# A two-block transformer layer stack on one core: the HGRN recurrence handled by halves of four heads

## The chip, the core and the metric

The kernel runs on one core of a Trainium2 chip. Its time is the device time of one execution in microseconds (us), the median over the runs shown. The engines are TensorE (PE), VectorE (DVE), ScalarE (ACT), GpSimd (POOL) and SyncE (SP); each works through its own queue in order and waits for the others at semaphores.

## What is computed

256 tokens of width 1024 in float32 pass through two blocks. Block 1 has two layers: a sparse attention (called DSA below) and an HGRN mixer, each followed by a residual layer norm and a SwiGLU feed-forward with its own layer norm. Block 2 (MIX) has gated linear attention beside latent attention, and a last feed-forward. The mixer around which the change is made, cut to what matters:

```
q, f, i, g = split(x @ w_in)                 # each 256 x 1024, 8 heads of 128
q  = silu(q);  fg = lb + (1 - lb) * sigmoid(f)
k  = 1 - fg;   logf = log(fg)
# per head, t the query's token, s <= t the key's:
b = cumsum(logf);  attn[t, s] = sum_d q[t, d] * exp(b[t, d] - b[s, d]) * k[s, d]
o = attn @ i  (+ what the state of earlier chunks adds)
o = rms_norm(o, g_norm) * silu(g)
return o @ w_o
rms_norm(x, g)      = x * rsqrt(mean(x*x) + eps) * g
layer_norm(x, g, b) = (x - mean) * rsqrt(var + eps) * g + b
```

## The kernel before, in words

The tokens are two tiles t = 0, 1 of 128 rows. Matrix products keep float32 accuracy by splitting each operand into a high part (`hi`, what the matmul's input format holds) and a low part (`lo`, the rest): `mm3` (L208 to L212) issues three matmuls, hi x hi (L210), hi x lo (L211) and lo x hi (L212). Weights come in units of 512 KB (`unit`, L183): SP issues the transfer into the ring `raw` of 4 buffers (L188), ACT rounds it into `rhi` (L174), and DVE (L176) or, for the names in `ON_POOL`, POOL in four pieces (L181) subtracts to get `rlo`. `rhi` and `rlo` have 9 buffers each. SP starts a transfer when a buffer of `raw` is free, in the order of use, so a held buffer holds up all weights behind it.

The stages in the order of time are DSA (to about 130 us of the span), the first feed-forward (to 327), HGRN (to about 500), the second feed-forward, MIX and the last feed-forward. Each stage is a string of steps (`HGRN`, `MIX`, ...) that `run` calls in turn; a scheduler then orders each engine's queue by its own estimates, so an edit in one place can reorder neighbours in another.

`hgrn_consts` (L696) runs beside the first feed-forward. It loads three tables through POOL's queue (L152) into buffers of the ring `raw`: `sel`, `lev`, and one that holds `msk`, `suf` and `id64`. DVE copies the last two out at L709 to L717, PE reads `sel` at L705.

In HGRN a projection step `P.x.t` is 8 `mm3` of 512 columns into one PSUM bank, evacuated by ACT or DVE. `l.t` takes logarithms of f and splits them; `t.t` forms q x k (`qk`, POOL, L761), sums it into the diagonal `dg` (L762), and turns q and k into `qT` and `kT` by PE transposes. `p.t.i` is a pair of heads: PE multiplies the logarithms with the table `lev` (L807, L808), ACT takes the exponential `e` (L810), and at each of the levels l = 0 to 6 the late halves of blocks of e are multiplied with `qT` (L817, DVE) and the early halves with `kT` (L819, DVE, or POOL at levels 2 and 5). PE then forms the products of a level (L824, L830), DVE places them under a mask into `blocks` (L835) and copies `attn` (L224), and PE multiplies by i (L846). The order before takes eleven projections, then the first pairs; five projections stand beside or between the eight pairs.

`rstd` (L254) makes 1/sqrt(scale x s + eps) on POOL in two instructions, a multiply-add (L257) and a power (L258). `rstd_halves` (L891) does it for a sum held in two parts, with two multiply-adds (L897, L898) and a power (L899); ACT squares the halves (L270) first, and DVE multiplies by the root at L910.

## Time and profile before

| | |
|---|---|
| median of 3 runs | 1157.36 us (1154.54 to 1159.5) |
| profiled execution, its own time | 1154.16 us |
| its span | 1152.4 us (1.76 us lie outside) |
| granted TensorE clock, mean | 0.989 of full speed |
| busy: PE, DVE, ACT, POOL | 1106.6, 697.3, 583.9, 224.3 us |

The profile is of one execution. Windows cut its span into stretches and give the busy time of each engine in them; a stretch less PE's busy time is PE's idle time there. The views of waits say which instruction an engine was waiting for, how long in total, how often, and the longest; a timeline shows each instruction with its start, its duration and, in brackets, the idle time of the engine just before it.

### The profile page before, as it was taken

The page shows a single profiled execution, that of the slowest core. Times are in us where ns is not written, and L with a number is a line of the kernel's source. Part 1 is how long each engine was busy: PE and PEld are TensorE (multiplying, and loading weights), DVE is VectorE, ACT ScalarE, POOL GpSimd, SP SyncE. Part 2 cuts the span into 40 slices and gives each one's busy share as a digit, 9 for nine tenths or more (in the row PEclk, how much of TensorE's full clock was granted, in tenths as well). Part 3 has the DMA queues.
Part 4 walks back from the last instruction along what each step waited for, and adds up shares of the span by engine and source line. Part 5 has one row for each costly group of instructions (what it writes and reads, how often), then busy time and mean ns, then how long its engine had stood idle before and what let it go on. Part 6 is the DMA issues. An engine that isn't in the chain of part 4 may idle for free.

```text
span 1152.4 us, 15343 instructions
## 1 busy us (share of the span) xinstructions
PE 1106.6 (96%) x5724; PEld 903.0 (78%) x5724; DVE 697.3 (61%) x1061; ACT 583.9 (51%) x832; POOL 224.3 (19%) x336
## 2 busy tenths in 40 slices
PE   8779999999999999999999999999999999999997
PEld 6546888878888777788888887887788878888886
DVE  6986755535566677875545486446655547454542
ACT  5656455525467466444444346763546456453441
POOL 2800620000432223200000022534100181000000
...
GB/s 250 159 85 5 243 166 229 182 119 255 146 146 173 103 145 77 119 214 180 218 183 192 175 131 174 207 159 102 164 192 146 146 146 225 174 222 202 171 140 37
DMA packets 98458, 187.33 MB, mean 163 GB/s; under 512 B 9400, under 2 KB 26952, under 8 KB 98384
## 3 DMA queue, kind: packets, MB, share of 16 engines
...
q14 instruction: 29, 0.24, 0.1%
HBM read 185.28 MB, written 1.05 MB: 162 GB/s over the span
## 4 chain that ended last, share of the span: by engine, by line
PE 81%; DVE 8%; POOL 4%; DMA 3%; issue 2%; ACT 2%; SPq 0%; POOLq 0%; DVEq 0%; ACTq 0%
PE a L210 15%; PE a L211 15%; PE a L212 15%; PE y L211 8%; PE y L210 8%; PE y L212 8%; PE t L236 3%; POOL rlo L181 2%; DVE rlo L176 1%; PE lv L830 1%; DMA raw<-in_ffn_w_up_dram 1%; DMA raw<-in_ffn_w_gate_dram 1%; DVE m L381 1%; ACT rhi L174 1%; PE L L538 1%
## 5 line engine op out<-in xcount | busy, mean ns | idle before, releaser
L176 DVE TENSOR_TENSOR rlo<-raw,rhi 128x1024 fp32r<-128x1024 f32 (+4 forms) x306 | 370.2, 1215 | 216.3 <-ACT rhi L174 204.8
L174 ACT ACTIVATE rhi<-raw 128x1024 fp32r<-128x1024 f32 (+3 forms) x338 | 352.7, 1047 | 242.8 <-PE y L212 75.5
L210 PE MATMUL a<-rhi,xh 128*128 128x512 f32 (+4 forms) x840 | 318.6, 379 | 3.4 <-ACT sil L625 1.8
L211 PE MATMUL a<-rlo,xh 128*128 128x512 f32 (+4 forms) x840 | 316.7, 377 | 0.2 <-DVE rlo L176 0.2
L212 PE MATMUL a<-rhi,xl 128*128 128x512 f32 (+4 forms) x840 | 315.4, 376 | 0.0
L210 PEld LDWEIGHTS a<-rhi,xh 128*128 128x128 f32 x840 | 158.7, 189 | 32.1 <-ACT xh L174 2.0
L211 PEld LDWEIGHTS a<-rlo,xh 128*128 128x128 f32 x840 | 158.8, 189 | 27.8 <-DVE rlo L176 0.6
L212 PEld LDWEIGHTS a<-rhi,xl 128*128 128x128 f32 x840 | 158.8, 189 | 27.4
L181 POOL TENSOR_TENSOR rlo<-raw,rhi 128x256 fp32r<-128x256 f32 x128 | 99.2, 811 | 179.8 <-ACT rhi L174 179.7
L210 PE MATMUL y<-rhi,hth 128*128 128x512 f32 x264 | 104.7, 396 | 0.5 <-ACT hth L174 0.5
L212 PE MATMUL y<-rhi,htl 128*128 128x512 f32 x264 | 103.2, 391 | 0.0
L211 PE MATMUL y<-rlo,hth 128*128 128x512 f32 x264 | 102.9, 390 | 0.0
L210 PE MATMUL y<-rhi,xh 128*128 128x512 f32 (+2 forms) x152 | 59.1, 390 | 3.1 <-ACT rhi L174 3.1
L257 POOL TENSOR_SCALAR rv<-mv 128x1 f32<-128x1 f32 x10 | 7.2, 716 | 272.0 <-DVE mv L266 271.8
L211 PE MATMUL y<-rlo,xh 128*128 128x512 f32 (+2 forms) x152 | 59.0, 388 | 1.0 <-POOL rlo L181 0.6
L212 PE MATMUL y<-rhi,xl 128*128 128x512 f32 (+2 forms) x152 | 58.6, 387 | 0.0
L174 ACT ACTIVATE hth<-t 128x512 fp32r<-128x512 f32 (+1 forms) x36 | 20.1, 558 | 75.6 <-PE t L236 75.6
L210 PEld LDWEIGHTS y<-rhi,hth 128*128 128x128 f32 x264 | 49.6, 188 | 10.7 <-ACT hth L174 1.1
L212 PEld LDWEIGHTS y<-rhi,htl 128*128 128x128 f32 x264 | 49.5, 188 | 10.6
L211 PEld LDWEIGHTS y<-rlo,hth 128*128 128x128 f32 x264 | 49.6, 188 | 9.7
L631 DVE TENSOR_TENSOR sil<-a,sil 128x512 f32<-128x512 f32 (+1 forms) x36 | 23.2, 643 | 51.1 <-PE a L212 51.0
L625 ACT ACTIVATE sil<-a 128x512 f32<-128x512 f32 (+1 forms) x36 | 20.2, 561 | 58.9 <-PE a L212 58.8
...
## 6 DMA issues: line engine op xcount, KB each, us to landing
...
```

The costliest lines, as they stand in the source:

```text
L174: self.nc.scalar.activation(hi, src, AF.Copy)
L176: self.nc.vector.tensor_sub(lo, src, hi.bitcast(F32))
L181: eng.tensor_sub(lo[:, c], src[:, c], hi[:, c].bitcast(F32))
L210: mm(out, xh, wh, start=start, stop=False)
L211: mm(out, xh, wl, start=False, stop=False)
L212: mm(out, xl, wh, start=False, stop=stop)
L236: self.nc.tensor.transpose(tp[:, j, :], b, self.ident)
L381: e2.tensor_tensor(m2, v[:, :, ::-1, :], s[:, None, :, :].to_broadcast(sh), ALU.mult)
L538: nc.tensor.matmul(L[:, j : j + 2, :], qT[t][:, g * 4 + (h0 + j) // 2, :], kT[:, g, :, :nk], start=False, stop=j == per - 2,)
L625: nc.scalar.activation(sil[ci, t][:, :cn], a[:, :cn], AF.Silu)
L631: nc.vector.tensor_mul(sil[ci, t][:, :cn], a[:, :cn], sil[ci, t][:, :cn])
L830: nc.tensor.matmul(lv[64 * c : 64 * c + 64, l - l0, j, :32], y, late, start=True, stop=True)
```

## The change

The recurrence is cut by halves n of four heads: logarithms, q x k and the transposes are steps of one (t, n). f and q of a half share one tile `fq`, and k and q transposed share one tile `QK`. At a level the two multiplies become one over the whole 128 tokens of each head: its second operand (`asked`) takes, every 64 >> l elements, k's and then q's values in turn from `QK`. All four logarithm steps stand together, pairs begin after eight projections, and one projection follows each pair. `h_k2`, `h_k5` and `hgrn_q1` leave `ON_POOL`, so the low parts of q1's four weight units go to DVE. The three tables of `hgrn_consts` go into tiles of the pool `w4` (10 buffers) instead of `raw`. In `rstd` the scale moves into ACT's squaring, the addition of eps to DVE in place; POOL keeps the power. In `rstd_halves` one DVE instruction adds both halves and eps.

```diff
@@ -251,12 +251,15 @@
         return X
 
 
-    def rstd(self, s, src, n, scale, eps):
-        v = self.sm(s, n, name="rv")
+    def root(self, s, v, n):
         r = self.sm(s, n, name="rs")
-        self.nc.gpsimd.tensor_scalar(v, src, scale, eps, ALU.mult, ALU.add)
         self.nc.gpsimd.tensor_tensor(r, v, self.nhalf[:, :n], ALU.pow)
         return r
+
+    def rstd(self, s, src, n, eps):
+
+        self.nc.vector.tensor_scalar(src, src, eps, None, ALU.add)
+        return self.root(s, src, n)
 
     def meanvar(self, s, views):
...
-    def sumsq(self, s, src, dst, junk):
-        self.nc.scalar.activation(junk[:, : src.shape[-1]], src, AF.Square, accum_out=dst)
+    def meansq(self, src, dst, junk, n):
+
+        self.nc.scalar.activation(junk[:, : src.shape[-1]], src, AF.Square, scale=n ** -0.5, accum_out=dst)
...
-        nc.scalar.activation(sq, o, AF.Square)
+        nc.scalar.activation(sq, o, AF.Square, scale=d ** -0.5)
...
-        raw = lambda: self.tile("raw", (P, 1024), F32, "raw")
-        sel = self.load(raw()[0:8, :], self.const("sel", 8)).rearrange("p (a b) -> p a b", a=8)
+        stage = [self.w4(name="stage") for _ in range(3)]
+        sel = self.load(stage[0][0:8, :], self.const("sel", 8)).rearrange("p (a b) -> p a b", a=8)
...
-        nc.vector.tensor_copy(lev, self.load(raw(), self.const("lev")))
+        nc.vector.tensor_copy(lev, self.load(stage[1], self.const("lev")))
         msk = self.w1(1, (P, 6, 32), mybir.dt.uint8, name="msk")
         o, n = OFF["msk"]
-        both = self.load(raw()[:, : n + P + 64], self.consts[:, o : o + n + P + 64])
+        both = self.load(stage[2][:, : n + P + 64], self.consts[:, o : o + n + P + 64])
...
+                both = self.w4(name="fq")
+                fg[t, n], q[t, n] = both[:, :512], both[:, 512:]
+                o = fg[t, n]
...
+        def logs(t, n):
+
+            if n not in lf:
+                lf[n] = (self.tile("rhi", (P, 2, 512), F32R, "lfh"), self.tile("rlo", (P, 2, 512), F32R, "lfl"))
+            x = self.w2(t, name="lf")
+            nc.scalar.activation(x, fg[t, n], AF.Ln)
+            self.halves(lf[n][0][:, t, :], lf[n][1][:, t, :], x)
+            nc.vector.tensor_scalar(fg[t, n], fg[t, n], -1.0, 1.0, ALU.mult, ALU.add)
+
+        def turned(t, n):
+
+            if n == 0:
+                dg[t] = self.sm(t, 8, name="dg")
+            both = QK[t, n] = self.w4((P, 2, 4, P), name="QK")
+            qk = self.w2(t, (P, 4, P), name="qk")
+            nc.gpsimd.tensor_tensor(qk.rearrange("p h d -> p (h d)"), q[t, n], fg[t, n], ALU.mult)
+            nc.vector.tensor_reduce(dg[t][:, 4 * n : 4 * n + 4], qk, AX.X, ALU.add)
+            self.copy(both[:, 1, :, :], self.blocksT(self.cols(q[t, n], 0, 4), "hT"), "h_qT")
+            self.copy(both[:, 0, :, :], self.blocksT(self.cols(fg[t, n], 0, 4), "hT"), "h_kT")
...
-            hs = slice(2 * i, 2 * i + 2)
+            hs, n, j0 = slice(2 * i, 2 * i + 2), i // 2, 2 * (i % 2)
+
+            def asked(l):
+
+                x = QK[t, n][:, 0, j0 : j0 + 2, :]
+                w = 64 >> l
+                return bass.AP(tensor=x.tensor, offset=x.offset, ap=[x.ap[0], [P, 2], [2 * w, 64 // w], [4 * P + w, 2], [1, w]])
...
-                    nc.vector.tensor_mul(part(y, l, 1), part(y, l, 1), part(qT[t][:, hs, :], l, 1))
-                    eng = nc.gpsimd if "h_k%d" % l in ON_POOL else nc.vector
-                    eng.tensor_tensor(part(y, l, 0), part(y, l, 0), part(kT[t][:, hs, :], l, 0), ALU.mult)
+                    y = y.rearrange("p j (b s e) -> p j b s e", s=2, e=64 >> l)
+                    nc.vector.tensor_tensor(y, y, asked(l), ALU.mult)
...
-        s2, v, r = self.sm(t, 2, name="s2"), self.sm(t, 2, name="rv"), self.sm(t, 1, name="rs")
+        s2, v = self.sm(t, 2, name="s2"), self.sm(t, 1, name="rv")
         for n in range(2):
-            self.sumsq(t, halves[n], s2[:, n : n + 1], self.w2(t, dt=BF16, name="sq"))
-        nc.gpsimd.tensor_scalar(v[:, 0:1], s2[:, 0:1], 1.0 / D, RMS_EPS, ALU.mult, ALU.add)
-        nc.gpsimd.tensor_scalar(v[:, 1:2], s2[:, 1:2], 1.0 / D, v[:, 0:1], ALU.mult, ALU.add)
-        nc.gpsimd.tensor_tensor(r, v[:, 1:2], self.nhalf[:, :1], ALU.pow)
-        return r
+            self.meansq(halves[n], s2[:, n : n + 1], self.w2(t, dt=BF16, name="sq"), D)
+        nc.vector.tensor_scalar(v, s2[:, 0:1], RMS_EPS, s2[:, 1:2], ALU.add, ALU.add)
+        return self.root(t, v, 1)
...
 WARM = 10
 PIECE = 256
 ON_POOL = {
-    "b2_g0", "b2_kn", "b2_vm", "b2_w_out", "dsa_o", "h_d", "h_k2", "h_k5", "hgrn_f0", "hgrn_q1", "rk0b",
+    "b2_g0", "b2_kn", "b2_vm", "b2_w_out", "dsa_o", "h_d", "hgrn_f0", "rk0b",
 }
 ON_ACT = {
     "d_k", "d_kT", "d_relu0", "d_relu1", "d_s0", "d_s1", "d_up00", "d_up10", "d_up11", "d_v", "h_g", "h_kT", "h_lb",
 HGRN = (
-    "P.f0.0 P.f1.0 Z P.f0.1 P.q0.0 P.q0.1 P.f1.1 P.q1.0 P.q1.1 l.1 l.0 t.0 P.i0.1 P.i0.0 P.i1.0 p.0.0 p.0.1 t.1 P.i1.1 "
-    "S P.g0.1 p.0.2 p.0.3 P.g0.0 p.1.0 p.1.1 g.0.0 p.1.2 p.1.3 P.g1.0 g.0.1 o.0.0 P.g1.1 g.1.0 o.1.0 g.1.1 o.0.1 n.0 "
-    "z.0 o.1.1 n.1"
+    "P.f0.0 P.f1.0 Z P.f0.1 P.f1.1 P.q0.0 P.q0.1 l.0.0 l.1.0 l.0.1 l.1.1 t.0.0 P.i0.0 P.i0.1 t.1.0 p.0.0 P.q1.0 p.0.1 "
+    "P.q1.1 S.0 p.1.0 P.i1.0 t.0.1 p.1.1 P.i1.1 t.1.1 p.0.2 P.g0.0 p.0.3 P.g0.1 S.1 p.1.2 P.g1.0 p.1.3 P.g1.1 "
+    "g.0.0 g.0.1 o.0.0 g.1.0 o.1.0 g.1.1 o.0.1 n.0 z.0 o.1.1 n.1"
```

Three places where the instructions now stand otherwise. First POOL in DSA, from the root of tile 0's index keys on (`mv` are their mean and variance, `rlo` the low parts of the output weights). Before:

```order
L257 TENSOR_SCALAR rv<-mv 128x1
L258 TENSOR_TENSOR rs<-rv,nhalf 128x1
L181 TENSOR_TENSOR rlo<-raw,rhi 128x256 x4
L257 TENSOR_SCALAR rv<-mv 128x1
L258 TENSOR_TENSOR rs<-rv,nhalf 128x1
L181 TENSOR_TENSOR rlo<-raw,rhi 128x256 x20
L152 DMA ln_g<-in_ln_g_dram 128x1024
L152 DMA ln_b<-in_ln_b_dram 128x1024
L181 TENSOR_TENSOR rlo<-raw,rhi 128x256 x8
```

After, POOL at the same place:

```order
L256 TENSOR_TENSOR rs<-mv,nhalf 128x1
L181 TENSOR_TENSOR rlo<-raw,rhi 128x256 x8
L256 TENSOR_TENSOR rs<-mv,nhalf 128x1
L181 TENSOR_TENSOR rlo<-raw,rhi 128x256 x22
L152 DMA ln_g<-in_ln_g_dram 128x1024
L152 DMA ln_b<-in_ln_b_dram 128x1024
L181 TENSOR_TENSOR rlo<-raw,rhi 128x256 x2
```

The second root stands behind eight pieces instead of four, and two pieces instead of eight follow the two transfers.

Second DVE within an early pair of HGRN. Before, the halves of a level are separate rows (L817, L819); after, a level is one row (L829), and the masked copy is L845. Before:

```order
L817 TENSOR_TENSOR e<-e,qT 128x2x16x4
L835 COPY_PREDICATED blocks<-msk,lv 128x8x8
L819 TENSOR_TENSOR e<-e,kT 128x2x16x4
L817 TENSOR_TENSOR e<-e,qT 128x2x32x2
L817 TENSOR_TENSOR e<-e,qT 128x2x64
L819 TENSOR_TENSOR e<-e,kT 128x2x64
L817 TENSOR_TENSOR e<-e,qT 128x2x64
L835 COPY_PREDICATED blocks<-msk,lv 128x16x4
L819 TENSOR_TENSOR e<-e,kT 128x2x64
L835 COPY_PREDICATED blocks<-msk,lv 128x32x2
```

After, DVE in an early pair:

```order
L829 TENSOR_TENSOR e<-e,QK 128x2x128 x4
L224 COPY attn<-lv 64x2x64
L845 COPY_PREDICATED blocks<-msk,lv 128x2x32
L829 TENSOR_TENSOR e<-e,QK 128x2x128
L845 COPY_PREDICATED blocks<-msk,lv 128x4x16
L829 TENSOR_TENSOR e<-e,QK 128x2x128
L845 COPY_PREDICATED blocks<-msk,lv 128x8x8
L829 TENSOR_TENSOR e<-e,QK 128x2x128
L845 COPY_PREDICATED blocks<-msk,lv 128x16x4
L845 COPY_PREDICATED blocks<-msk,lv 128x32x2
```

The pair has seven multiplies on DVE instead of twelve, and none on POOL.

Third DVE at the entry of MIX for tile 1 (x is the residual, h its normed copy that PE turns next). Before:

```order
L283 SCALAR_TENSOR_TENSOR x_120<-x_120,rs,ln_b 128x512 x2
L908 TENSOR_TENSOR h<-x_120,pre_mix 128x512 x2
L176 TENSOR_TENSOR rlo<-raw,rhi 128x960
L910 TENSOR_SCALAR h<-h,rs 128x512 x2
L959 SCALAR_TENSOR_TENSOR lr<-a,rs,vec_b 128x384
```

After, DVE at the same entry:

```order
L176 TENSOR_TENSOR rlo<-raw,rhi 128x960
L261 TENSOR_SCALAR mv<-mv 128x1
L286 SCALAR_TENSOR_TENSOR x_120<-x_120,mv,ln_g 128x512 x2
L287 SCALAR_TENSOR_TENSOR x_120<-x_120,rs,ln_b 128x512 x2
L916 TENSOR_TENSOR h<-x_120,pre_mix 128x512 x2
L907 TENSOR_SCALAR rv<-s_6040 128x1
L918 TENSOR_SCALAR h<-h,rs 128x512 x2
```

The sum for the root (L907) is DVE's own work directly ahead of its use, and the low part of the weights has moved ahead of the norm.

## Rows read from the trace of the kernel before

**Rows 1.** The page, part 1: engine, busy us, share of the span, instructions

```profile
PE 1106.6 (96%) x5724; PEld 903.0 (78%) x5724; DVE 697.3 (61%) x1061; ACT 583.9 (51%) x832; POOL 224.3 (19%) x336
```

**Rows 2.** The page, part 4: the chain that ended last, shares by engine

```profile
PE 81%; DVE 8%; POOL 4%; DMA 3%; issue 2%; ACT 2%; SPq 0%; POOLq 0%; DVEq 0%; ACTq 0%
```

**Rows 3.** Windows by stage: length, busy us of each engine (instructions), granted clock, DMA

```profile
0.00:130.00 130.00, 109.41 (x584) 81.08 (x585) 102.26 (x240) 76.33 (x173) 39.46 (x61) 0.96 0.44 138
130.00:360.00 230.00, 225.14 (x1065) 186.94 (x1064) 123.01 (x144) 115.15 (x134) 56.73 (x95) 0.99 0.55 178
360.00:500.00 140.00, 134.44 (x997) 109.62 (x996) 108.61 (x250) 75.18 (x101) 35.90 (x53) 0.98 0.41 135
```

**Rows 4.** Waits of PE, 228 to 290 us: total us, times, longest

```profile
PE t L236 <- DVE sil L631: 2.1, 1, 2.1
PE a L210 <- ACT sil L625: 1.8, 1, 1.8
```

**Rows 5.** Windows of three stretches, columns as in rows 3

```profile
242.00:248.00 6.00, 5.01 (x17) 4.11 (x18) 2.14 (x4) 1.66 (x2) 0.00 (x0) 0.72 0.31 91
380.00:480.00 100.00, 95.00 (x809) 76.78 (x807) 75.95 (x212) 52.19 (x74) 32.73 (x49) 0.97 0.31 103
390.00:404.00 14.00, 12.85 (x91) 10.05 (x92) 9.32 (x23) 5.79 (x9) 5.10 (x8) 0.76 0.08 18
```

**Rows 6.** Timeline of POOL, 225 to 262 us: start, duration, what, [idle before]

```profile
225.39 0.56 POOL L152 DMA_DIRECT2D raw<-in_consts_dram  x1 [8.63 <-DVE rlo L176]
```

**Rows 7.** Timeline of the SP queue, 225 to 262 us

```profile
234.52 25.61 SPq L188 DMA_DIRECT2D raw<-in_ffn_w_gate_dram  x6
```

**Rows 8.** Timeline of DVE, 261 to 262.5 us

```profile
261.91 0.68 DVE L709 CAST lev<-raw 128x1024 fp32r<-128x1024 f32 x1
```

**Rows 9.** Waits of PE, 390 to 482 us

```profile
PE lv L824 <- DVE e L819: 1.5, 1, 1.5
```

**Rows 10.** DVE by form, 320 to 500 us: busy us, mean ns, idle

```profile
L176 DVE TENSOR_TENSOR rlo<-raw,rhi 128x1024 fp32r<-128x1024 f32 x38 | 45.9, 1218 | 6.1 <-ACT rhi L174 5.9
L817 DVE TENSOR_TENSOR e<-e,qT 128x128 f32<-128x128 f32 x56 | 18.7, 343 | 4.0 <-ACT e L810 3.9
L819 DVE TENSOR_TENSOR e<-e,kT 128x128 f32<-128x128 f32 x40 | 13.2, 330 | 0.0
```

**Rows 11.** Lines L814, L817 and L819, 320 to 500 us: duration ns min/median/max

```profile
L814 DVE TENSOR_TENSOR e<-e,qT x4: 406/415/683, 440.1 to 464.6; 128x256 f32<-128x256 f32 x4
...
L817 DVE TENSOR_TENSOR e<-e,qT x56: 273/283/1255, 381.3 to 463.7; 128x128 f32<-128x128 f32 x56
...
L819 POOL TENSOR_TENSOR e<-e,kT x16: 447/518/1765, 381.9 to 460.7; 128x128 f32<-128x128 f32 x16
```

**Rows 12.** Waits of PE, 500 to 1153 us

```profile
PE t L236 <- DVE h L910: 3.3, 3, 1.5
```

**Rows 13.** Timeline of POOL, 690 to 698 us

```profile
691.59 2.13 POOL L897 TENSOR_SCALAR rv<-s 128x1 f32<-128x1 f32 x1 [1.18 <-ACT sq L270]
...
694.81 0.56 POOL L899 TENSOR_TENSOR rs<-rv,nhalf 128x1 f32<-128x1 f32 x1
```

**Rows 14.** Timeline of POOL, 24 to 130 us

```profile
30.66 2.91 POOL L181 TENSOR_TENSOR rlo<-raw,rhi 128x256 fp32r<-128x256 f32 x4 [1.34 <-ACT rhi L174]
...
33.96 0.55 POOL L258 TENSOR_TENSOR rs<-rv,nhalf 128x1 f32<-128x1 f32 x1
...
54.67 5.54 POOL L181 TENSOR_TENSOR rlo<-raw,rhi 128x256 fp32r<-128x256 f32 x8
```

**Rows 15.** Timeline of DVE, 30 to 40 us

```profile
34.99 0.36 DVE L467 SCALAR_TENSOR_TENSOR ki<-ki,rs,vec_a 128x128 f32<-128x128 f32 x1
```

**Rows 16.** Timeline of DVE, 52 to 66 us

```profile
54.69 4.94 DVE L381 TENSOR_TENSOR m<-up,sin 128x128 f32<-128x128 f32 x1
```

**Rows 17.** Line L381, 30 to 70 us, columns as in rows 11

```profile
L381 DVE TENSOR_TENSOR m<-up,sin x8: 277/282/4944, 33.7 to 66.7; 128x128 f32<-128x128 f32 x8
```

**Rows 18.** Timeline of PE, 60 to 61 us

```profile
60.42 0.90 PE L236 MATMUL t<-ident,up 128*128 128x128 f32 x3 [3.96 <-DVE up L382]
```

More of the change, by code (lines that the diff above doesn't have):

```diff
@@ L278, in ln_residual @@
         mv = self.meanvar(t, [X[:, 0:512], X[:, 512:1024]])
-        r = self.rstd(t, mv[:, 1:2], 1, 1.0, LN_EPS)
+        r = self.rstd(t, mv[:, 1:2], 1, LN_EPS)
         for n in range(2):
@@ L439, in inA @@
             n = self.w1(t, name="cqn")
-            self.sumsq(t, a[:, :256], ss, n)
-            r = self.rstd(t, ss, 1, 1.0 / 256, RMS_EPS)
+            self.meansq(a[:, :256], ss, n, 256)
+            r = self.rstd(t, ss, 1, RMS_EPS)
             nc.vector.scalar_tensor_tensor(n, a[:, :256], r, gcq, ALU.mult, ALU.mult)
@@ L459, in inB @@
             mv = self.meanvar(t, [a[:, 128:256]])
-            r = self.rstd(t, mv[:, 1:2], 1, 1.0, LN_EPS)
+            r = self.rstd(t, mv[:, 1:2], 1, LN_EPS)
             vs[t] = keep[t][:, 0:128]
@@ L742, in evac @@
                 nc.vector.scalar_tensor_tensor(o, o, 2.0 ** -64, u, ALU.max, ALU.subtract)
-        def logs(t):
-            lf[t] = (self.tile("rhi", (P, D), F32R, "lfh"), self.tile("rlo", (P, D), F32R, "lfl"))
-            for n in range(2):
-                c = slice(n * 512, (n + 1) * 512)
-                x = self.w2(t, name="lf")
-                nc.scalar.activation(x, fg[t][:, c], AF.Ln)
-                self.halves(lf[t][0][:, c], lf[t][1][:, c], x)
-                nc.vector.tensor_scalar(fg[t][:, c], fg[t][:, c], -1.0, 1.0, ALU.mult, ALU.add)
@@ new lines, in hgrn, with state @@
+        S = [None]
+        def state(n):
+            if n == 0:
+                S[0] = self.w4((P, 8, P), name="S")
+            a = self.bank("hE")
+            nc.tensor.matmul(a, suf, lf[n][0][:, 0, :], start=True, stop=False)
+            nc.tensor.matmul(a, suf, lf[n][1][:, 0, :], start=False, stop=True)
+            e = self.w2(0, name="e")
+            nc.scalar.activation(e, a, AF.Exp)
+            nc.vector.tensor_mul(e, e, fg[0, n])
+            a = self.bank("hS", (P, 4, P))
+            for j in range(4):
+                nc.tensor.matmul(
+                    a[:, j, :], e[:, j * P : (j + 1) * P], v[0][:, n * 512 + j * P : n * 512 + (j + 1) * P],
+                    start=True, stop=True,
+                )
+            self.copy(S[0][:, n * 4 : n * 4 + 4, :], a, "h_S")
@@ L956, in low_rank @@
             c = self.w2(t, (P, n * P), name="lr")
[L957 to L958 removed]
+            self.meansq(a, ss, c, n * P)
+            r = self.rstd(t, ss, 1, RMS_EPS)
             nc.vector.scalar_tensor_tensor(c, a, r, row[:, : n * P], ALU.mult, ALU.mult)
```

61 lines of the change are left out of this document (16 added, 45 removed).

## The prediction

> **What bounds the kernel now.** I read the busy times first: PE is busy for 1106.6 us of 1152.4, 96%, and no other engine is above 61% [rows 1]. The chain that ended last is PE's for 81% [rows 2]. So the time is what PE issues plus what it loses, and since the change leaves the number of PE's multiplies of weights as it was, only the losses can move: 45.8 us of idle time (1152.4 less 1106.6), and stretches at the lower clock, where PE is busy but slow. The windows by stage come next [rows 3]. Idle is 20.6 us in DSA (130 less 109.41), 4.9 in the first feed-forward, and 5.6 in the stretch of HGRN. The change touches all three and, through `rstd`, each place where one stage hands over to another. For each stall the view of waits names the instruction that PE stood for; I then follow that instruction to its own cause in the timelines.
>
> **The first feed-forward.** PE waits twice between 228 and 290 us, 2.1 us for DVE's gated product and 1.8 us for ACT's silu [rows 4], and its clock falls after the first: the mean is 0.72 of full speed over the 6 us from 242 [rows 5], so 0.28 x 6 = 1.7 us are lost. The cause begins 17 us earlier. POOL starts the load of the first table at 225.39 into a buffer of `raw` [rows 6], and two more follow within 9 us. They hold three of the ring's four buffers until DVE has copied `lev` out at 261.91 [rows 8]; meanwhile the weights pass through the one that is left, and SP needs 25.61 us for six units [rows 7], 4.3 us each. ACT's and DVE's conversions come late for that reason. With the tables in `w4` the ring keeps its four buffers, SP runs ahead, and POOL's loads wait for nothing. All of it goes: 2.1 + 1.8 + 1.7 = 5.6 us. If the stalls had another cause the gain is 0; if the weights arrive earlier still, nothing more can be won here, since this stretch holds only 4.9 us of idle in all.
>
> **The pairs of HGRN.** PE waits 5.6 us between 380 and 482, most of it for DVE's multiplies and copies (the largest single wait is 1.5 us for L819 [rows 9]; the sum is that of the stretch's idle time [rows 3]). The granted clock is 0.76 over the 14 us from 390 [rows 5]: 0.24 x 14 = 3.4 us. Together 9.0 us. The first pairs stand there with no projection beside them, and PE's 64-row products wait on a chain exponential, two multiplies, product, masked copy.
>
> The work on DVE: L817 and L819 take 18.7 + 13.2 = 31.9 us [rows 10], and POOL does 16 early halves besides (median 518 ns) [rows 11]. After, 56 multiplies of 128 x 256. The nearest row is L814, the same shape with the query part alone, at 406 to 683 ns, median 415 [rows 11]. Its second operand is contiguous; the new one hops from k to q. Upper bounds from rows: two halves at the median of 283 ns each, 0.57 us, or, if collisions were the rule, the longest L817 of 1.255 us [rows 11]. I take 0.415: 56 x 0.415 = 23.2 us. The four units of low parts that come from POOL cost 4 x 1.218 = 4.9 us [rows 10]. DVE's net is 23.2 + 4.9 - 31.9 = -3.8 us, beside 24.05 us that it was idle in the 100 us from 380 [rows 5], so DVE stays under the limit and the 4.9 us lie beside PE's projections.
>
> At the last level but the diagonal the second operand changes between k and q at every element. Before, the same level read every other element, and none of the 56 L817 is told apart by it: the minimum is 273 and the median 283 ns [rows 11]. The Trainium skill speaks against the merged form (Vector Engine (DVE) Microarchitecture Reference, section 5.2, Measured stream behaviour on trn2): one source that hops at every element streams at 1.73 ns a column instead of 1.05, while runs of two adjacent words keep the full rate. By the Trainium skill's figures eight of the 56 would be longer by 256 x 0.68 ns = 0.17 us, an estimate, 1.4 us of DVE in all; the sum would not notice it.
>
> What is gained at PE is not DVE's 3.8 us but the waits. With a projection after each pair, PE has 24 matmuls to issue while a pair's chain runs, so the clock should not fall: 3.4 us. Of the waits I leave some: eight pairs with about 0.4 us each, 3.2, and one collision of DVE with a long POOL instruction (POOL still forms q x k and scales the output) at 1.3, the longest L817. That is 4.5 us left of 9.0, so 4.5 us gained. Bounds: 9.0, and none.
>
> **The roots.** PE waits three times, 3.3 us, for h, the normed residual at the entries of MIX and of the last feed-forward [rows 12]. At 691.59 the first of POOL's two multiply-adds takes 2.13 us, the second and the power follow to 695.37 [rows 13]. After, DVE adds by itself right behind its product h and POOL has the power of 0.56 us left, so the root is ready about 2 us earlier; the largest of these waits is 1.5. All 3.3 us go. The price is a small DVE instruction for each root, beside other work. Bounds: 1.5 (one of the waits stays covered only in part) to 3.3.
>
> **DSA.** This stage is a chain through DVE and ACT, and reordering hits it on both sides. Against: four pieces take 2.91 us, and the second root ended at 34.51 [rows 14], just ahead of DVE's use of it at 34.99 [rows 15]. Behind eight pieces it ends at 30.66 + 5.8 + 0.55 = 37.0, 2.0 us too late, and the ropes of the index keys queue behind that DVE instruction. For: one rope multiply, L381, took 4.944 us where the median of eight is 0.282 [rows 17]; it began at 54.69 [rows 16], as POOL began the eight pieces behind the two transfers [rows 14], and PE then waited 3.96 us [rows 18]. After, only two pieces stand there. The Trainium skill (SBUF - State Buffer, section SBUF: two separate sides) has DVE with two inputs and POOL take turns at a shared port, each for a whole instruction. By that the wait would be one piece, 0.73 us by the row; the row shows several, so the trace agrees on the collision and not on its length. The ends are +2.0 (the long one comes back elsewhere) and 2.0 - 4.0 = -2.0. The median multiply escaped, so I go nearer to the second: -1.0.
>
> **The sum.** -5.6 - 4.5 - 3.3 - 1.0 = -14.4 us. Against the profiled execution's own time, 1154.16, that is 1139.8. That execution lies 3.2 us under the median of the runs shown, 1157.36, so the forecast against the median is 1143.
>
> **Rivals.**
> The pairs gain nothing: waits change their names, because DVE's queue now carries low parts between the multiplies of a pair (1.22 us each, in front of products that PE needs) and POOL's long products remain. For it: DVE is 76% busy there [rows 5], and its queue is in order. Against: 24 us of DVE idle. Then the time is 1143 + 4.5 = 1147.5.
> DSA gives back: the root is late and a long collision comes again, +2.0 instead of -1.0: 1146. For it: POOL's train of 22 pieces is longer than any before. Against: fewer pieces stand where the long one was.
> The first feed-forward's stalls stay, since the tables were not their cause: 1143 + 5.6 = 1148.6. Against it: SP's row of 25.61 us has no other holder of buffers. Two of these three together give 1150.5 to 1153, all three 1156, which is no change.
> Slower: the merged multiply is far from its row. At the 1.255 us of the longest L817, the 56 take 70.3 us, DVE has 70.3 + 4.9 - 31.9 = 43.3 us more to do in a stretch with 24.05 free, and PE waits for the other 19.3. With the other gains, 9.9, the time is 1157.4 - 9.9 + 19.3 = 1166.8. It decides from about 0.91 us a multiply, where DVE is full, and makes the kernel slower than before from 1.09. Only collisions with POOL gave such times so far, and POOL loses its 16 early halves, so I hold it unlikely.
>
> **How the numbers follow.** The forecast has 0.55, the pairs alone 0.12, DSA alone 0.08, the feed-forward alone 0.04, two or three of them 0.15, slower 0.06. Of this kernel's runs a change of 0.5%, 5.8 us, can be told from none: faster is under 1151.6, slower over 1163.1. The forecast's own range is 1137.5 (all 9.0 us of the pairs, DSA's better end) to 1148 (the roots' lower bound, DSA's worse end). The first three rivals are faster singly, their sums mostly not, so faster 0.80, same 0.14, slower 0.06. The range that leaves out 2 in 10 is 1136 to 1153: 1.5 us under the forecast's own for the spread between runs, and up to the costliest two rivals together.
>
> **What would show it.** In the first feed-forward SP issues six units in about the time of six uses, and the clock from 242 reads 1.00. The merged multiply has a median under 0.45 us; PE's waits between the first and the last pair sum to under 5 us, and no window there has a clock under 0.95. At MIX's entries PE no longer waits for h. In DSA, DVE waits about 2 us for the second root, and no rope takes over 1.5 us. I am wrong if the pairs still lose 9 us, if DSA's stretch is longer by over 2 us, or if feed-forwards that the change does not touch move by more than a microsecond or two.

## The result, and the profile after

The change makes the kernel slower, by about 0.6%: 1163.25 us median of 5 runs (1159.44 to 1164.11) against 1157.27 of before, ratio 1.0057, 95% interval 1.0032 to 1.0082. The forecast was 1143. The profiled execution took 1164.11 us, its span is 1162.3 us and its mean granted clock 0.982 of full speed.

To see where the time went I cut every profiled execution at the same matmuls: the hi x hi product (L210 in `mm3`) occurs 1422 times in the same order in all kernels, and its 1st, 97th, 385th, 505th and 1417th lie near the borders of the stages. Times in us:

| run | 1st at | DSA | first FFN | HGRN | rest | own time | ratio to before, 95% |
|---|---|---|---|---|---|---|---|
| before | 10.2 | 122.0 | 202.3 | 146.6 | 659.2 | 1154.2 | |
| after | 11.6 | 131.8 | 197.4 | 149.2 | 660.5 | 1164.1 | 1.0057 (1.0032 to 1.0082) |
| dsa_back | 10.3 | 122.6 | 195.8 | 149.5 | 661.0 | 1152.7 | 0.9974 (0.9953 to 0.9996) |
| dsa_cq_back | 10.0 | 125.3 | 197.4 | 146.5 | 659.9 | 1152.7 | 0.9989 (0.9968 to 1.0011) |
| dsa_ki_back | 11.7 | 130.1 | 197.4 | 148.0 | 660.4 | 1161.2 | 1.0060 (1.0033 to 1.0087) |
| keep_on_dve | 11.3 | 126.3 | 195.8 | 151.1 | 661.5 | 1159.7 | 1.0000 (0.9976 to 1.0024) |
| roots_only | 10.9 | 131.0 | 202.0 | 144.6 | 660.0 | 1162.1 | 1.0038 (1.0016 to 1.0059) |
| consts_only | 10.5 | 122.9 | 198.1 | 148.1 | 659.0 | 1152.4 | 0.9974 (0.9958 to 0.9990) |
| hgrn_only | 10.9 | 122.5 | 199.5 | 147.3 | 658.9 | 1152.9 | 0.9995 (0.9975 to 1.0015) |
| two_multiplies | 10.2 | 123.0 | 197.5 | 146.3 | 661.1 | 1151.7 | 0.9941 (0.9916 to 0.9965) |
| table_early | 10.4 | 122.6 | 197.4 | 145.8 | 660.3 | 1150.0 | 0.9929 (0.9902 to 0.9956) |
| state_early | 11.3 | 124.3 | 195.8 | 147.9 | 661.3 | 1154.1 | 1.0005 (0.9981 to 1.0029) |
| old_order | 10.8 | 122.8 | 195.8 | 141.2 | 660.6 | 1144.8 | 0.9889 (0.9858 to 0.9919) |
| old_order_two | 10.6 | 121.5 | 195.8 | 147.1 | 661.4 | 1150.0 | 0.9962 (0.9941 to 0.9984) |
| old_order_early | 10.1 | 123.5 | 195.8 | 141.2 | 663.0 | 1147.1 | 0.9926 (0.9901 to 0.9951) |
| exp_q1 | 9.8 | 122.3 | 197.4 | 146.0 | 659.8 | 1148.9 | 0.9960 (0.9942 to 0.9978) |
| silu_first | 11.4 | 124.0 | 195.8 | 151.2 | 660.8 | 1156.8 | 0.9989 (0.9967 to 1.0012) |
| silu_first_early | 10.8 | 122.5 | 195.8 | 145.6 | 660.6 | 1148.8 | 0.9969 (0.9951 to 0.9988) |
| staged_best | 9.5 | 122.5 | 197.4 | 144.2 | 660.8 | 1148.4 | 0.9945 (0.9924 to 0.9966) |
| staged_best2 | 10.3 | 124.1 | 197.4 | 141.4 | 661.0 | 1147.8 | 0.9918 (0.9889 to 0.9947) |

A ratio compares medians on one chip; a stretch is of one execution. Five kernels have the same HGRN code (after, the two after dsa_back, dsa_back itself and keep_on_dve) and show 146.5 to 151.1 there, so a single figure of that column carries about 2 us either way. DSA is steadier: the fifteen executions whose DSA has its roots as before show 121.5 to 124.3. The profiled executions of after and before differ by 9.9 us, the medians by 6.0. By stretches: start +1.4, DSA +9.8, first FFN -4.9, HGRN +2.6, rest +1.3.

The page of after, part 1 (engine, busy us, share, instructions), to be held against [rows 1]:

```profile
PE 1115.6 (96%) x5724; PEld 907.9 (78%) x5724; DVE 699.4 (60%) x1057; ACT 585.3 (50%) x834; POOL 183.8 (16%) x264
```

PE has the same 5724 instructions and is busy 9.0 us longer, with the mean clock at 0.982 instead of 0.989: more of them ran at the lower clock.

**First FFN.** PE's waits in after, 130 to 330 us (total, times, longest), and SP's queue there:

```profile
PE a L210 <- ACT xh L174: 0.2, 1, 0.2
```

```profile
236.30 18.49 SPq L188 DMA_DIRECT2D raw<-in_ffn_w_gate_dram  x6
```

The two waits of [rows 4] are gone, and six units take 18.49 us where they took 25.61 [rows 7]. The lower clock is gone at 242, but 3.4 us of it stand at 270 instead, where PE waits for nothing (window: length, busy PE, PEld, DVE, ACT, POOL, granted clock):

```profile
268.00:275.00 7.00, 7.00 (x31) 5.74 (x31) 2.71 (x6) 1.77 (x3) 0.00 (x0) 0.76 0.84 272
```

So of the 4.9 us 4.3 are idle time and 0.6 busy time.

**DSA.** ACT's timeline (start, duration, what, idle before), first of before, then of after, which starts 1.4 us later:

```profile
25.63 0.28 ACT L222 ACTIVATE k<-y 128x128 f32<-128x128 f32 x1 [0.26 <-DVE cqn L442]
...
33.50 0.28 ACT L222 ACTIVATE keep<-y 128x128 f32<-128x128 f32 x1
33.66 0.61 ACT L228 ACTIVATE up<-y 128x512 f32<-128x512 f32 x1
35.16 0.60 ACT L222 ACTIVATE qiT<-t 128x512 f32<-128x512 f32 x1 [0.90 <-PE t L236]
```

```profile
23.71 0.38 ACT L274 ACTIVATE cqn<-y 128x256 f32<-128x256 f32 x1
...
29.30 1.06 ACT L174 ACTIVATE rhi<-raw 128x1024 fp32r<-128x1024 f32 x1 [2.45 <-DMA raw<-in_att_w_uq_dram]
30.26 0.58 ACT L228 ACTIVATE up<-a 128x512 f32<-128x512 f32 x1
31.39 1.06 ACT L174 ACTIVATE rhi<-raw 128x1024 fp32r<-128x1024 f32 x1 [0.55 <-DMA raw<-in_att_w_o_dram]
32.36 0.26 ACT L222 ACTIVATE k<-y 128x128 f32<-128x128 f32 x1
...
38.87 0.60 ACT L228 ACTIVATE up<-y 128x512 f32<-128x512 f32 x1 [1.54 <-PE y L212]
...
41.53 0.60 ACT L222 ACTIVATE qiT<-t 128x512 f32<-128x512 f32 x1 [1.11 <-PE t L236]
42.02 0.27 ACT L222 ACTIVATE keep<-y 128x128 f32<-128x128 f32 x1
```

Two things make tile 1's copy `k` late. It follows DVE's product `cqn`: in before it waits 0.26 us for it. That product is late itself; DVE of before, then of after:

```profile
25.11 0.49 DVE L442 SCALAR_TENSOR_TENSOR cqn<-y,rs,vec_a 128x256 f32<-128x256 f32 x1 [0.34 <-POOL rs L258]
```

```profile
26.22 0.15 DVE L261 TENSOR_SCALAR ss<-ss 128x1 f32<-128x1 f32 x1
...
28.68 0.48 DVE L446 SCALAR_TENSOR_TENSOR cqn<-y,rs,vec_a 128x256 f32<-128x256 f32 x1
```

ACT's sum of squares is there at 24.18, but the new addition (L261) stands in DVE's queue behind low parts until 26.22, and the product behind others until 28.68. Then `k` stands in ACT's queue behind two conversions that wait for weights (2.45 and 0.55 us) and runs at 32.36; in before at 25.63. `keep` of tile 1 moves from 33.50, ahead of `up` and `qiT`, to 42.02, behind both. What waits for them, DVE and PE of after:

```profile
42.33 0.17 DVE L468 TENSOR_SCALAR wi<-y 128x8 f32<-128x8 f32 x1 [2.10 <-ACT keep L222]
```

```profile
35.61 1.09 PE L236 MATMUL y<-ident,kd 128*128 128x128 f32 x4 [2.17 <-DVE kd L456]
...
37.35 0.63 PE L210 MATMUL y<-rhi,cq 128*128 128x512 f32 x1
...
43.41 0.39 PE L210 MATMUL y<-rhi,cq 128*128 128x512 f32 x1
...
68.78 1.08 PE L236 MATMUL y<-ident,up 128*128 128x128 f32 x4 [3.49 <-DVE up L386]
```

Windows of after (columns as above), the first of the whole stretch:

```profile
11.60:143.40 131.80, 112.93 (x570) 84.77 (x570) 98.74 (x241) 73.00 (x168) 33.87 (x49) 0.89 0.37 117
...
36.00:41.00 5.00, 5.00 (x17) 3.92 (x16) 3.65 (x11) 2.14 (x3) 5.00 (x9) 0.50 0.54 204
```

Behind the wait of 2.17 us PE works at half clock, 1.2 GHz: a product of 512 columns takes 0.63 us instead of 0.39. In before the same stretch has 105.96 us of PE busy in 122.0, at 0.96, for the same 570 matmuls. So of the 9.8 us 7.0 are longer busy time, which goes with the lower clock, and 2.8 idle time. Two parts of this are not followed to a cause: the clock's first rise comes 2.6 us later in after, as it does in some of the runs with DSA's roots as before, and most of the lower clock stands behind the wait of 3.49 us (0.67 from 70 us and 0.55 from 80, in windows of 10 us), whose chain is not traced back to `k` and `keep` step by step.

**HGRN.** PE's waits in after, 323 to 510 us, and two windows:

```profile
PE y L786 <- DVE e L783: 2.7, 1, 2.7
PE lv L840 <- DVE e L829: 2.1, 2, 1.4
PE lv L834 <- DVE e L829: 0.9, 1, 0.9
```

```profile
400.00:410.00 10.00, 8.46 (x77) 6.18 (x76) 6.18 (x20) 1.09 (x2) 1.40 (x3) 0.83 0.08 33
450.00:460.00 10.00, 7.29 (x49) 5.84 (x48) 5.54 (x14) 4.36 (x7) 2.45 (x4) 0.88 0.41 153
```

DVE ahead of each of the two longest waits, with POOL beside the first:

```profile
398.95 1.25 DVE L261 TENSOR_SCALAR ss<-ss 128x4 f32<-128x4 f32 x1
400.11 0.41 DVE L829 TENSOR_TENSOR e<-e,QK 128x256 f32<-128x256 f32 x1
401.44 0.69 DVE L300 TENSOR_TENSOR fq<-o,rs 128x512 f32<-128x512 f32 x1 [0.91 <-POOL rs L256]
402.05 0.42 DVE L829 TENSOR_TENSOR e<-e,QK 128x256 f32<-128x256 f32 x1
...
454.38 0.23 DVE L945 CAST suf<-raw 128x128 fp32r<-128x128 f32 x1 [2.04 <-DMA raw<-in_consts_dram]
454.52 0.16 DVE L261 TENSOR_SCALAR ss<-ss 128x4 f32<-128x4 f32 x1
455.83 0.69 DVE L300 TENSOR_TENSOR fq<-o,rs 128x512 f32<-128x512 f32 x1 [1.15 <-POOL rs L256]
456.44 0.68 DVE L783 TENSOR_TENSOR e<-e,fq 128x512 f32<-128x512 f32 x1
```

```profile
398.58 1.59 POOL L767 TENSOR_TENSOR qk<-fq 128x512 f32<-128x512 f32 x1 [2.40 <-DVE ss L298]
```

The pair's multiply (L829) and the state's (L783) stand behind the norm of an earlier pair, which waits about 1 us for POOL's power, and the second also behind a table of MIX that is still on its way. By the window of the whole stretch PE is idle for 6.6 us at a clock of 0.98; in before it is 5.6 us of 146.6, at 0.98:

```profile
340.80:490.00 149.20, 142.58 (x1022) 114.24 (x1021) 99.85 (x208) 86.06 (x114) 25.79 (x35) 0.98 0.40 132
```

The merged multiply itself (count, ns min/median/max; then busy us, mean ns, DVE's idle time before it):

```profile
L829 DVE TENSOR_TENSOR e<-e,QK x56: 409/419/1035, 373.3 to 472.0; 128x256 f32<-128x256 f32 x56
```

```profile
L829 DVE TENSOR_TENSOR e<-e,QK 128x256 f32<-128x256 f32 x56 | 22.4, 439 | 15.6 <-ACT e L821 15.6
```

**Rest.** PE's waits in after from 510 us on:

```profile
PE t L236 <- DVE h L918: 2.3, 3, 1.2
...
PE y L236 <- DVE ss L261: 1.1, 1, 1.1
PE a L210 <- ACT kg L222: 1.1, 1, 1.1
```

The waits for h are 1.0 us shorter than in [rows 12]; two others of 1.1 us stand beside them, one of them (L261) by the view for an addition that the change gave to DVE. The norm of tile 1 at MIX's entry, DVE of before and then of after:

```profile
695.40 0.88 DVE L910 TENSOR_SCALAR h<-h,rs 128x512 f32<-128x512 f32 x2 [1.73 <-POOL rs L899]
```

```profile
703.50 0.88 DVE L918 TENSOR_SCALAR h<-h,rs 128x512 f32<-128x512 f32 x2 [0.69 <-POOL rs L256]
```

From the end of the product h to this line it is 2.80 us in before (692.60 to 695.40) and 0.92 in after (702.58 to 703.50). But in before DVE makes a low part of 1.15 us in that time, which in after stands ahead of the norm; DVE's idle time falls by 1.0 us only.

### The profile page after: what moved, and what is told of

Read it like the earlier page. It is cut to its first block, busy times and chain, and to the rows that moved or that the text cites. A ratio compares the mean times of both kernels' runs of the same rounds, so it can differ in the third digit from the quotient of the medians.

```text
span 1162.3 us, 15241 instructions
## 1 busy us (share of the span) xinstructions
PE 1115.6 (96%) x5724; PEld 907.9 (78%) x5724; DVE 699.4 (60%) x1057; ACT 585.3 (50%) x834; POOL 183.8 (16%) x264
## 5 line engine op out<-in xcount | busy, mean ns | idle before, releaser
L176 DVE TENSOR_TENSOR rlo<-raw,rhi 128x1024 fp32r<-128x1024 f32 (+3 forms) x310 | 379.4, 1229 | 212.0 <-ACT rhi L174 199.7
L210 PE MATMUL a<-rhi,xh 128*128 128x512 f32 (+4 forms) x840 | 318.4, 379 | 2.2 <-ACT xh L174 1.1
L210 PEld LDWEIGHTS a<-rhi,xh 128*128 128x128 f32 x840 | 158.7, 189 | 30.7 <-ACT xh L174 2.1
L181 POOL TENSOR_TENSOR rlo<-raw,rhi 128x256 fp32r<-128x256 f32 x112 | 86.5, 807 | 178.2 <-ACT rhi L174 174.2
L210 PE MATMUL y<-rhi,hth 128*128 128x512 f32 x264 | 104.6, 396 | 0.5 <-ACT hth L174 0.5
L210 PE MATMUL y<-rhi,xh 128*128 128x512 f32 (+2 forms) x152 | 59.7, 394 | 3.2 <-ACT rhi L174 3.2
L210 PEld LDWEIGHTS y<-rhi,hth 128*128 128x128 f32 x264 | 49.6, 188 | 10.6 <-ACT hth L174 1.1
L635 DVE TENSOR_TENSOR sil<-a,sil 128x512 f32<-128x512 f32 (+1 forms) x36 | 23.2, 644 | 55.4 <-PE a L212 55.4
L256 POOL TENSOR_TENSOR rs<-mv,nhalf 128x1 f32<-128x1 f32 x10 | 9.0, 897 | 290.3 <-DVE mv L261 290.3
```

What stands on the lines that cost most here:

```text
L176: self.nc.vector.tensor_sub(lo, src, hi.bitcast(F32))
L181: eng.tensor_sub(lo[:, c], src[:, c], hi[:, c].bitcast(F32))
L210: mm(out, xh, wh, start=start, stop=False)
L256: self.nc.gpsimd.tensor_tensor(r, v, self.nhalf[:, :n], ALU.pow)
L635: nc.vector.tensor_mul(sil[ci, t][:, :cn], a[:, :cn], sil[ci, t][:, :cn])
```

## The experiments

The expectations name their theories by letters; the text says in words which held.

**dsa_back**: after, with both roots of DSA as before.

```
-            r = self.rstd(t, ss, 1, RMS_EPS)
+            r = self.rstd_old(t, ss, 1, 1.0 / 256, RMS_EPS)
-            r = self.rstd(t, mv[:, 1:2], 1, LN_EPS)
+            r = self.rstd_old(t, mv[:, 1:2], 1, 1.0, LN_EPS)
```

> The changed kernel with the four roots of DSA made as before (two POOL instructions each), all else as changed. Theory A: in DSA the new roots let the scheduler move ACT's copies for tile 1 (k, keep) behind weight conversions, and that costs 8 to 11 us; so this kernel is at 1152 to 1155, and DSA's first output matmul stands at 76 to 78 us as before, not at 89. Theory B: the profiled executions differ by chance at the start (the clock's first rise comes 2.6 us later in one) and in HGRN; then this kernel gains under 3 us, 1160 or more.

DSA goes back to 122.6 and the ratio falls to 0.9974. The roots of DSA, which move one small instruction each from POOL to DVE (for cq also a factor into ACT's squaring), cost the 9 us. The next two put back one of the two edits each, cq's root (the first pair of lines) and the index keys'.

> The changed kernel with only the root of cq in DSA made as before (the index keys' root stays new). ACT's queue then has tile 1's k copy where it was before, ahead of the weight conversions. Theory A (the place of ACT's small copies sets DSA): most of the 9 to 10 us come back, DSA's output matmuls start near 78 us, the time is 1151 to 1154 on this chip. Theory C (the second index-key root behind eight POOL pieces, the forecast's reason): it still stands there, so no more than 2 us come back, 1158 or more.

> The changed kernel with only the index keys' root in DSA made as before (the root of cq stays new). Theory A: ACT's order stays the late one, so 7 us or more of the loss stay: 1158 to 1161 on this chip. Theory C: the loss was this root's place on POOL, and the time falls to 1152 or less.

With cq's root back DSA takes 125.3 and ACT's `k` stands at 25.49, with the index keys' back 130.1 and 30.74; both medians, 1153.07 and 1160.6, are in the ranges of theory A. The main loss is cq's root. The 3.3 us that remain over before are not the late second root, for which DVE waits 0.60 us here: PE's waits for `up` sum to 11.1 us instead of 7.8, the longest 6.0. Ahead of it a rope multiply (L394, the one with cos) ran long, as in [rows 16]:

```profile
55.93 5.03 DVE L394 TENSOR_TENSOR m<-up,cos 128x128 f32<-128x128 f32 x1
```

**keep_on_dve**: after, with the two late copies of tile 1 on DVE.

```
-            self.copy(vs[t], a[:, 0:128], "d_v")
+            self.copy(vs[t], a[:, 0:128], "d_v" if t == 0 else "dve")
```

(and `d_k` in the same way.)

> The changed kernel, new roots everywhere, with two small copies of tile 1 in DSA (k and the kept v, 128 x 128 each) taken from ACT and given to DVE. Theory A: what is late in ACT's queue no longer holds tile 1's keys, DVE does not wait 2.1 us for the kept copy, and 5 us or more of DSA's loss come back. If the scheduler's order of the rest (up, kT, cq behind conversions) is what costs, only 2 to 4 us do.

126.3, 5.5 us less than after, with the new roots in place, and although a rope multiply of 4.93 us is back: ACT's two copies carry over half of the loss. DVE of this run then shows what stood hidden behind `keep`:

```profile
40.24 0.81 DVE L471 SCALAR_TENSOR_TENSOR ki<-ki,rs,vec_a 128x128 f32<-128x128 f32 x1 [2.42 <-POOL rs L256]
```

That is the forecast's late second root, 2.42 us, here behind twelve pieces on POOL where the forecast had eight.

**roots_only**, **consts_only**, **hgrn_only**: before with one part of the change each (all roots; the three `stage` tiles; `HGRN`, `ON_POOL` and the mixer's functions).

> The kernel before with the new roots everywhere and nothing else. Theory A: DSA is 8 to 11 us longer, the entries of MIX and of the last feed-forward gain at most 1 us (the trace shows their waits for h at 2.3 instead of 3.3): 1165 to 1167. Theory B (chance at the start): under 1160.

> The kernel before with the three tables staged in w4 and nothing else. Theory A: the first feed-forward loses its two waits and its stretch at the lower clock, 4.9 us by the comparison of the two traces, 5.6 by the forecast: 1152. Theory B: without HGRN's new order the ring of w4 is held otherwise, and SP or POOL waits elsewhere: within 2 us of before.

> The kernel before with the recurrence by halves, its order and the merged multiply, without the new roots and the staged tables. Theory A (HGRN itself costs): 2 to 3 us slower than before in the stretch of HGRN, 1160, PE still waiting for DVE, where DVE waits for a transfer in its own queue. Theory B (the forecast's term, hidden by the new roots' longer round trip between DVE and POOL): 3 to 5 us faster, 1153.

The roots alone lengthen DSA by 9.0 us in the profiled execution, which is what theory A says, and make the kernel slower (1.0038), less than the 1165 to 1167 of that theory. The median, 1159.46, is 4.4 us over before's on its chip; that is under the 1160 set for theory B, so the time alone does not decide and the stretches do. PE's idle time in HGRN is 3.6 us there instead of 5.6. The tables alone take 4.2 us off the first FFN, all but 0.4 of it idle time. The recurrence alone changes nothing that can be told (0.9995), which neither expectation had.

**two_multiplies**: dsa_back with the merged multiply as two on DVE again.

```
-                    nc.vector.tensor_tensor(y, y, asked(l), ALU.mult)
+                    nc.vector.tensor_mul(part(y, l, 1), part(y, l, 1), part(qk[:, 1, j0 : j0 + 2, :], l, 1))
+                    eng.tensor_tensor(part(y, l, 0), part(y, l, 0), part(qk[:, 0, j0 : j0 + 2, :], l, 0), ALU.mult)
```

> The run dsa_back with each level's merged multiply undone into two on DVE (112 of 128 x 128 instead of 56 of 128 x 256, about 32 us of DVE instead of 23). If the merged multiply helps the pairs, PE's waits for e grow and the stretch of HGRN is 1 to 4 us longer than the 149.5 us of dsa_back. If DVE's free time covers it (it is idle 30% of the pairs), it stays within 1 us, and the merging is worth nothing at PE.

146.3, 3.2 us shorter than dsa_back's single figure and within the spread of that code: no gain by the merge can be seen in the new order.

**table_early**: dsa_back with MIX's table (`suf64`, the DMA that DVE waited 2.04 us for) loaded in the first FFN into a tile of its own. **state_early**: that, and `S.1` ahead of `P.g0.0`.

> The changed kernel with DSA's roots as before (the run dsa_back) and MIX's suffix table loaded ahead into a tile of its own. Theory D: in HGRN's second state step DVE stands 2.0 us for this table's transfer, then adds eps, waits 1.2 us for the root, and only then makes the product that PE waits 2.2 to 2.7 us for; so this wait falls under 1 us and the stretch of HGRN, 149.5 us there, is 2 to 3.5 us shorter. Theory E: the order itself costs (64-row products interleaved with projections); then the stretch stays within 1 us.

> The run table_early (new order) with the second half's state step moved from just ahead of the pair that needs it to before the two pairs in front. Theory E' (the new order puts steps with a chain PE - ACT - DVE - PE where no projection covers them): PE's wait of 1.2 us for the state's product goes, the stretch of HGRN is 1 to 2 us shorter than 145.8. Rival (the clock alone sets the differences between these stretches): only the granted clock changes and the waits stay as they are.

The wait for the state falls from 2.2 to 1.2 us and the stretch to 145.8. With the state earlier its wait is gone, but those of the pairs grow from 3.0 to 4.8 us (five), and the stretch is 147.9: waits moved. By ratio state_early is 0.8% behind table_early, more than these stretches show; the two ran on different chips, and the difference stays unexplained.

**old_order**: dsa_back with the steps in before's order, by halves.

```
-    "P.f0.0 P.f1.0 Z P.f0.1 P.f1.1 P.q0.0 P.q0.1 l.0.0 l.1.0 l.0.1 l.1.1 t.0.0 P.i0.0 P.i0.1 t.1.0 p.0.0 P.q1.0 p.0.1 "
+    "P.f0.0 P.f1.0 Z P.f0.1 P.q0.0 P.q0.1 P.f1.1 P.q1.0 P.q1.1 l.1.0 l.1.1 l.0.0 l.0.1 t.0.0 t.0.1 P.i0.1 P.i0.0 P.i1.0 "
+    "p.0.0 p.0.1 t.1.0 t.1.1 P.i1.1 S.0 S.1 P.g0.1 p.0.2 p.0.3 P.g0.0 p.1.0 p.1.1 g.0.0 p.1.2 p.1.3 P.g1.0 g.0.1 o.0.0 "
...
```

> The run dsa_back with the steps of HGRN in the order of before (both halves of a step called one after the other), the merged multiply and the half tiles kept. Theory E (the order costs): the stretch of HGRN comes to 146.6 us or less, that of before. Theory D: it stays near 149 unless the wait for MIX's table happens to move.

141.2, and 1144.32 us median (ratio 0.9889), the fastest version. On the same chip table_early and two_multiplies took 1149.92 and 1149.77. PE's waits, 300 to 495 us, and the whole stretch:

```profile
PE t L236 <- POOL fq L890: 0.7, 1, 0.7
PE lv L844 <- DVE e L839: 0.7, 1, 0.7
...
PE y L796 <- DVE e L793: 0.5, 1, 0.5
```

```profile
329.40:470.60 141.20, 138.93 (x1023) 113.17 (x1021) 99.95 (x209) 83.99 (x112) 31.18 (x35) 1.00 0.43 136
```

PE is idle for 2.3 us and its clock stays full; dsa_back, with the other order and the same 1023 matmuls, has 5.9 us idle and 143.62 busy, at 0.97. Not all of that busy time is the clock's: two_multiplies and exp_q1 (below) have the new order and no lower clock in this stretch, and PE is still busy for 142.64 and 141.26 us. The window of two_multiplies:

```profile
330.60:477.00 146.40, 142.64 (x1023) 112.25 (x1022) 104.21 (x264) 86.36 (x114) 25.88 (x35) 1.00 0.42 134
```

**old_order_two**, **old_order_early**: old_order with the two multiplies, and with the early table.

> The run old_order with the merged multiply undone into two on DVE. Theory G (in an order that covers DVE's chain the merging is worth nothing at PE): the stretch of HGRN stays within 1.5 us of old_order's 141.2, and the time near 0.989 to 0.991 of before. Theory H (the merging is what made old_order shorter than the kernel before): the stretch goes back to 143 to 146 us.

> The best version so far by its parts: old_order with MIX's suffix table loaded ahead. In old_order PE waits only 0.5 us for the state step's product, so by theory D little is left: within 2 us of old_order, 0.987 to 0.990 of before. If the table still holds DVE somewhere that PE waits for, 1 to 2 us better.

Two multiplies cost 5.9 us of the stretch in the old order (147.1, over the 143 to 146 expected; PE waits 2.0 and 1.3 us for them): there the merge gains, 4.2 us by the medians of old_order_two and old_order_early, which ran on one chip (1150.93 and 1146.77). The early table changes nothing (141.2 again); its ratio, 0.9926, misses the 0.987 to 0.990 expected, was taken on another chip than old_order's and overlaps it.

**exp_q1**, **silu_first**, **silu_first_early**: the new order puts q1's Silu between the pairs, and ACT then loads function tables (1.283 us each) between exponentials. exp_q1 leaves out q1's Silu, whose place an Exp takes; silu_first moves `P.q1.0 P.q1.1` ahead of the logarithms; the third adds the early table.

> The kernel of dsa_back (new order of HGRN's steps), with one change: the queries of heads 4 to 7 (projections q1, which stand between the first pairs) go through Exp instead of Silu, so their values are left out of what is computed; the number of instructions stays. In the new order ACT changes its function table between Exp (for the pairs) and Silu (for q1) and back: the profile of after has 17 ACT_TABLE_LOAD of 1.283 us in HGRN where before has 14, four of them between the first and the fourth pair, and DVE waited 15.6 us there for ACT's e (5.4 in old_order). Theory J: these table changes, with the exponentials queued behind them, are what the new order of steps costs at its first pairs. Then four loads go (36 to 32 in the program), DVE's wait for e falls from about 15 to under 9 us, and the stretch of HGRN from 149.5 (dsa_back) to 142 to 145. Rival K: the order of PE's products and projections costs it, whatever ACT's tables; then the stretch stays at 147 to 150 and the ratio at 0.997.

> dsa_back with P.q1.0 and P.q1.1 moved ahead of the logarithms, so that ACT's Silu for the queries is done before the first exponential, and nothing else moved: the pairs p.0.0, p.0.1 and p.1.0 then stand with no projection between them. Theory J (ACT's table changes between the pairs are what costs): four table loads fewer, the stretch of HGRN falls to 142 to 145 although its first pairs lose two projections, ratio about 0.992. Rival K (a projection after each pair is what keeps PE busy, and ACT's tables are beside the point): the stretch stays at 147 to 150 or grows, and PE's waits for e at the first pairs grow from the 3.0 us that the new order shows.

> silu_first with MIX's table loaded during the first feed-forward, as in table_early. Theory J with the table's wait (2.0 us of DVE, seen in after at 454 us, in front of the second state): 1 to 3 us less than silu_first in HGRN's stretch, 141 to 143, about as old_order (141.2). If old_order is better for another reason than ACT's tables and this wait, the stretch stays above 145.

146.0, 151.2 and 145.6, where 141 to 145 would have borne the theory out. DVE's wait for e falls, from 16.6 us in dsa_back to 13.5, 9.5 and 6.8, and PE's loss does not follow it. The function tables are a small part of the cause at most.

**staged_best**, **staged_best2**: before with the tables staged, the roots outside DSA and MIX's table early; the second leaves the low-rank norms' roots as before.

> A version from the parts that gained: the kernel before, its HGRN unchanged, with the tables staged, the new roots outside DSA only, and MIX's suffix table loaded ahead (one 64 KB tile of its own, loaded beside the first feed-forward), so that DVE does not wait for it within the pairs. By theory A: tables -4 to -5, roots in HGRN -2, entries of MIX 0 to +1: 1149 to 1151 where before is 1155 to 1157. If the new roots cost outside DSA too: 1152 or more.

> The run staged_best (0.9945 of before) with the two low-rank norms of MIX taking their roots as before. There PE waited 1.1 us for a transposed row behind DVE's new add and 1.0 us for a low part; both waits were not there before. Theory F (a small add in DVE's queue that waits for ACT holds up what is behind it): these two go, MIX's entry is 0.5 to 2 us shorter, 0.993 to 0.994 of before. Rival: they move to POOL's longer chain and the entry is unchanged.

0.9945 and 0.9918, on different chips, with HGRN's steps and its two multiplies as in before. Its stretch, 144.2 and 141.4, shows that the merge is not the only way to old_order's 141.2. In the second the wait for L261 is gone, but at the entry of MIX another of 1.1 us stands in its place, and the rest takes 661.0 us against 660.8, unchanged as the rival has it.

```profile
PE y L236 <- DVE lr L972: 1.1, 1, 1.1
```

## Why the prediction was wrong

The forecast for the profiled execution was 1139.8, and it took 1164.1. Of these 24.3 us, by stretches and rounded, DSA has 10.8, the pairs 7.1, the rest 4.6, the start 1.4 and the first FFN 0.7.

**First FFN, -5.6: right in its waits, partly luck in its size.** -4.9 in after, -4.2 to -6.5 in the runs with the tables staged. The two waits, 3.9 us of the forecast, are gone, and the rival that the tables were not the cause falls. The 1.7 us of clock were not gained in after, since 3.4 us at half clock stand at 270; consts_only has them at 260 without a wait, and hgrn_only, which keeps the waits, has none. What sets that stretch is open. A detail of the reading was off: one of the three buffers came free at 253.6, with the copies of `msk`, `suf` and `id64`, not at 261.91.

**DSA, -1.0 between ends of 2.0: here the sign was lost; measured +9.8.** The step that failed is "The ends are +2.0 (the long one comes back elsewhere) and 2.0 - 4.0 = -2.0": both look at the index keys' root and at the collision alone. The root of cq, which the change splits over DVE and POOL as well, stands in the sum at nothing; with it back DSA falls from 131.8 to 125.3. Both effects that I named are there. The second root is late, 2.42 us once ACT no longer hides it (keep_on_dve). The long collision is gone in after: the longest L385 (before's L381) takes 0.868 us instead of 4.944 [rows 17], by the line's durations in after:

```profile
L385 DVE TENSOR_TENSOR m<-up,sin x8: 267/280/868, 38.5 to 67.9; 128x128 f32<-128x128 f32 x8
```

So the better end's gain came in after, and the +9.8 are what is left of a larger loss. When cq's root goes by DVE and then POOL, its addition and product stand in DVE's queue behind other work, and tile 1's copies on ACT stand behind conversions that wait for weights; I read neither place. The rival that DSA gives back had +2.0 by the late root, not this. It had the collision's return right for dsa_cq_back and keep_on_dve, where eight pieces stand behind the two transfers again.

**Pairs, -4.5: the price was right, the cover was not; measured +2.6, which the spread of about 2 us does not tell from nothing.** The 56 multiplies take 22.4 us where I had 23.2. Two of the last levels of one pair, on DVE, the second that with the hop:

```profile
430.37 0.42 DVE L829 TENSOR_TENSOR e<-e,QK 128x256 f32<-128x256 f32 x1
...
430.83 0.48 DVE L829 TENSOR_TENSOR e<-e,QK 128x256 f32<-128x256 f32 x1
```

By the Trainium skill (Vector Engine (DVE) Microarchitecture Reference, section 5.2) the last level's hopping operand would add 0.17 us, an estimate; the eight such multiplies take 0.477 to 0.504 us against the median of 0.419, so the trace agrees on the direction and shows under half the size. The slower rival, 0.91 us a multiply and more, falls. What failed is "With a projection after each pair ... the clock should not fall". It falls to 0.83 and 0.88 in two windows, and the stretch loses no less than before: 6.6 us idle and a clock of 0.98, against 5.6 and 0.98. A gain by the merge shows only in the old order, 5.9 us by the stretch. The rival "waits change their names" came nearest: DVE's in-order queue does hold the pair's multiplies, behind a norm and a copy that wait at the two longest stalls, not behind the low parts that I named. The chance of 0.06 for a slower kernel was given to the multiply's price; the kernel is slower by DSA instead, whose loss had no price in the forecast.

**Roots at the entries, -3.3: not gained; measured +1.3 for the whole rest.** The root is ready about 2 us earlier after its product, as forecast (0.92 instead of 2.80 us). The step that failed is "All 3.3 us go": 1.15 us of that time had been filled with a low part, which now stands ahead, so PE's waits for h fall by 1.0 us and waits of 1.1 us appear beside them.

Left open: which part of the new order of steps costs what. Against old_order it costs dsa_back 8.3 us by the stretch, 3.6 of them idle time and 4.7 busy time, of which the lower clock is only a part, and table_early and two_multiplies some 5.5 us by the medians on one chip; moving the state, the table or the Silu projections did not bring back more than the spread. The parts' ratios (roots +0.4%, tables -0.3%, recurrence 0) sum to +0.1% where the whole shows +0.6%; with intervals of 0.2% about each, some tenths of a percent stay unexplained. Also open is DSA's long collision: old_order, the fastest version, still has a rope multiply of 4.96 us.
